# All 64 norms of a two-layer trunk: the epsilon added by ScalarE behind its Square, GpSimd left with the power

## The chip, the cores and the metric

The kernel runs on one core of a Trainium2 chip. The metric is the device time of one execution in microseconds (us), from start to end on that core. Each kernel is timed several times, and its median counts. A profiled execution gives the trace. Its span, from the first to the last recorded instruction, is slightly shorter than its device time. The engines are TensorE (PE, with its weight loads PEld), VectorE (DVE), ScalarE (ACT), GpSimd (POOL) and SyncE (SP), whose queue issues nearly all transfers.

## The reference

The reference is a trunk of two layers over x of shape (1, 1024, 1024) in float32, that is 1024 tokens of width 1024. Each layer is a mixer and a SwiGLU feed-forward network (FFN), and each of the four sub-layers has a norm ahead and a norm behind it:

```python
def rmsnorm(x, g):
    y = x * lax.rsqrt(jnp.mean(x * x, axis=-1, keepdims=True) + 1e-6)
    return y * g
# every sub-layer
x = x + rmsnorm(f(rmsnorm(x, g_pre)), g_post)
# layer 0: f = attention_mixer (8 heads chunked softmax, 8 heads stick-breaking, out-projection), then swiglu
# layer 1: f = recurrent_mixer (gated linear recurrence with a conv), then swiglu
def swiglu(h, w_gate, w_up, w_down):
    return (jax.nn.silu(h @ w_gate) * (h @ w_up)) @ w_down
```

The matrix products are made to float32 accuracy. The norms need, for each token, one number: (mean of squares + epsilon) to the power -1/2.

## The kernel before

**Tiles.** The 1024 tokens are eight tiles of 128 tokens, one token per partition, in the text "token 0" to "token 7". A norm of one tile makes a column of 128 numbers. With four sub-layers, two norms each and eight tiles, there are 64 such norms.

**One norm.** `rstd` (L170 to L184) computes it in three steps on two engines. ACT squares the tile with a scale of 1/32 and sums along the free axis into a column `ss` (L178; a second short instruction, ACTIVATION_READ_ACCUMULATOR, puts the sum out). POOL adds the epsilon, `rs` = `ss` + eps (L182). POOL raises `rs` to the power -0.5, with an exponent from a constant column `neghalf` (L183). In the last sub-layer four of the norms come in two halves of 512 columns. There the first half's sum gets the epsilon at L180, on POOL, and L182 adds the first half's column to the second's. `self.squared` names the last Square. Work that is to be issued behind a norm is tied to it (`last_m`, `behind`).

**Who uses it.** In `pre_norm` the normalized tile is either made by DVE together with the gain (L214, the attention's norm at the start, into `h`) or by ACT (L212, into `mg` or `m`; the gain is folded into the weights). Eight PE transposes of 128x128 then turn it (L222), and `sink.take` splits the result into a high and a low part (L57 and L58 into `hT` for a mixer, L85 to L96 into `hS` and `tf` for an FFN). In `post_norm_of` DVE multiplies the sub-layer's result by its gain (L250), and then one DVE instruction forms x = result * rs + x (L256). The new x is stored (L258) and, but for the last sub-layer, goes on into the next sub-layer's `pre_norm`.

**Stages.** The start normalizes and turns eight tiles of x while the attention's weights come in (PE L291 and L293 are its first products, on `psv`). At the end of a mixer the out-projection works through tokens 0 to 5 in threes and 6 and 7 at the end. The post-norms and the FFN's pre-norms of tokens 6 and 7 stand there between the last products and the first products of the FFN. The FFN's gate and up projections use Strassen's seven products (L604 to L661, tiles `q`, `c`, `first`). The down projection has six block products (L726 to L733 work on splits `o` of `raw` loads) and then a seventh over four tiles of tokens (L833 loads its weights `raw`; L842 and L843 split the loads `act`, which are small pieces of a stored activation `gA`). L848 ends it, tile by tile, and the post-norms of its two token groups run beside these products. The tile pools have few buffers (`act` 2, `x` 2, `rs` 4, `ss` 4), so a transfer into one waits until the former user is done.

**Order.** A scheduler sets the order of instructions on each engine, with a cost for each instruction and a simulated timeline. A changed instruction can therefore move others on all engines. Within an engine the order is fixed at build time, and each instruction waits for its inputs.

## Time and profile before

| | before |
|---|---|
| median of 3 runs | 2243.35 us (2241.7 to 2243.67) |
| profiled execution | 2241.47 us |
| its span | 2239.6 us |
| mean granted clock of PE | 0.995 |
| POOL, busy in the span | 227.3 us, 458 instructions |
| L183, the power, 64 times | 46.5 us, 727 ns each |

A row of the timeline reads: start in us, duration in us, engine, line, operation, output <- inputs (buffer numbers left out), how many in a row. In square brackets stand the idle time of the engine just before and what ended it. A row of a group reads: line, engine, operation, names, shapes, count, then busy us in total, the mean in ns, and the idle time before with its releasers. A row of PE's waits reads: what PE wanted, what it waited for, us in total, how many times, the longest. L numbers are lines of the kernel before.

### The profile page before, as it was taken

Reading aid. Unit: us, or ns where it says so; the run is one execution under the profiler, and the core shown is the slowest. Engines: PE = TensorE matmul, PEld = TensorE weight load, DVE = VectorE, ACT = ScalarE, POOL = GpSimd, SP = SyncE. Lnnn points to the kernel's source line nnn. Section 1 sums busy time; section 2 is a strip of 40 time slices with the busy share of each in tenths; the row PEclk is TensorE's granted clock in tenths of the full one; section 3 lists DMA queues with packets and bytes.
Section 4 is the critical chain, followed back from the end, with each engine's and each line's share of the span. In section 5 each row is a group of like instructions: output and inputs, shape, how many; then the busy total and the mean of one; then the engine's idle time right before and its main releaser. Section 6 shows DMA issues by size and latency. Waiting matters only on the chain. (4 is left out here: it accounts for less than half of the span.)

```text
span 2239.6 us, 30733 instructions
## 1 busy us (share of the span) xinstructions
PE 2194.9 (98%) x11198; PEld 1806.9 (81%) x11198; DVE 1539.4 (69%) x2496; ACT 1146.0 (51%) x2108; POOL 227.3 (10%) x458
## 2 busy tenths in 40 slices
PE   8999999999999999999999999999999999999997
PEld 8887888878788888888887777888788888888875
DVE  5776765464877777776767677437786777759665
ACT  4544455464765444432436576528655444425433
POOL 2111212131100000000001332202000000000011
PEclk9999999999999999999999999999999999999998
DMA  5101011125523323235558411356232323237466
GB/s 168 47 27 36 25 43 41 60 98 169 183 76 113 118 90 123 90 132 201 161 168 252 131 57 48 92 195 227 75 128 98 123 90 123 90 126 259 127 202 193
DMA packets 185978, 268.92 MB, mean 120 GB/s; under 512 B 13794, under 2 KB 115170, under 8 KB 185827
## 3 DMA queue, kind: packets, MB, share of 16 engines
q1 hardware_dynamic: 185186, 264.86, 37.5%
q10 hardware_dynamic: 640, 2.10, 0.3%
q8 instruction: 88, 1.44, 0.3%
q14 instruction: 64, 0.52, 0.1%
HBM read 201.38 MB, written 65.54 MB: 119 GB/s over the span
## 5 line engine op out<-in xcount | busy, mean ns | idle before, releaser
L646 PE MATMUL ps<-hS,q 128*128 128x512 f32 (+1 forms) x1288 | 489.7, 381 | 0.7 <-ACT hS L96 0.3
L647 PE MATMUL ps<-hS,q 128*128 128x512 f32 (+1 forms) x1288 | 489.0, 380 | 0.9 <-DVE hS L89 0.9
L648 PE MATMUL ps<-hS,q 128*128 128x512 f32 (+1 forms) x1288 | 488.4, 380 | 0.0
L617 DVE TENSOR_TENSOR q<-raw,q 128x512 fp32r<-128x512 f32 x308 | 204.5, 685 | 185.7 <-ACT q L616 185.2
L647 PEld LDWEIGHTS ps<-hS,q 128*128 128x128 f32 x1288 | 242.1, 188 | 47.5 <-DVE hS L89 1.3
L646 PEld LDWEIGHTS ps<-hS,q 128*128 128x128 f32 x1288 | 241.7, 188 | 47.8 <-ACT hS L96 0.7
L648 PEld LDWEIGHTS ps<-hS,q 128*128 128x128 f32 x1288 | 242.1, 188 | 45.8
L616 ACT CAST q<-raw 128x512 fp32r<-128x512 f32 x308 | 177.3, 616 | 154.7 <-DVE raw L625 127.6
L732 PE MATMUL ps<-o,o 128*128 128x512 f32 x616 | 241.6, 393 | 3.3 <-DVE o L727 3.2
L733 PE MATMUL ps<-o,o 128*128 128x512 f32 x616 | 238.8, 392 | 0.0
L731 PE MATMUL ps<-o,o 128*128 128x512 f32 x616 | 222.2, 395 | 10.1 <-ACT o L842 6.0
L604 ACT ACTIVATE raw<-raw,gcol 128x256 f32<-128x256 f32 x352 | 150.2, 498 | 151.8 <-DMA raw<-in_ffn_w_up_dram 73.2
L726 ACT CAST o<-raw 128x512 fp32r<-128x512 f32 x206 | 123.8, 620 | 197.7 <-PE ps L733 63.8
L727 DVE TENSOR_TENSOR o<-raw,o 128x512 fp32r<-128x512 f32 x206 | 138.0, 687 | 64.3 <-ACT o L726 63.4
L182 POOL TENSOR_SCALAR rs<-ss 128x1 f32<-128x1 f32 x60 | 33.1, 551 | 1451.5 <-ACT junk L178 1367.8
L731 PEld LDWEIGHTS ps<-o,o 128*128 128x128 f32 x616 | 116.2, 189 | 38.9 <-ACT o L842 8.5
L156 DVE TENSOR_TENSOR wlo<-raw,whi 128x1024 fp32r<-128x1024 f32 x76 | 93.1, 1225 | 71.5 <-ACT whi L155 70.1
L732 PEld LDWEIGHTS ps<-o,o 128*128 128x128 f32 x616 | 116.7, 189 | 29.5 <-DVE o L727 5.3
L733 PEld LDWEIGHTS ps<-o,o 128*128 128x128 f32 x616 | 116.6, 189 | 24.6 <-DVE o L843 0.7
L155 ACT CAST whi<-raw 128x1024 fp32r<-128x1024 f32 x76 | 79.7, 1051 | 58.7 <-PE ps L167 20.2
L401 ACT COPY pt<-tr 128x512 f32<-128x512 f32 (+1 forms) x128 | 65.5, 527 | 78.6 <-PE tr L397 78.0
L166 PE MATMUL psq<-hT,whi 128*128 128x512 f32 x256 | 101.2, 395 | 1.1 <-DVE v L296 1.1
(201 smaller groups left out, 4303.4 us busy)
## 6 DMA issues: line engine op xcount, KB each, us to landing
raw<-in_ffn_w_down_dram SPq DMA_DIRECT2D x96, 256.0 KB, 4.4
raw<-in_ffn_w_gate_dram SPq DMA_DIRECT2D x44, 512.0 KB, 4.2
raw<-in_ffn_w_up_dram SPq DMA_DIRECT2D x44, 512.0 KB, 4.2
gS<-c SPq DMA_DIRECT2D x88, 256.0 KB, 3.7
raw<-gS SPq DMA_DIRECT2D x88, 256.0 KB, 2.8
gA<-c SPq DMA_DIRECT2D x66, 256.0 KB, 3.5
raw<-in_attn_w_in_dram SPq DMA_DIRECT2D x24, 512.0 KB, 4.1
raw<-gA SPq DMA_DIRECT2D x44, 256.0 KB, 2.9
```

Source lines behind the costliest of these rows:

```text
L166: nc.tensor.matmul(ps, wh[:, kt, cols], hh[:, kt, :], start=kt == 0, stop=False)
L604: nc.scalar.activation(raw[:, i], raw[:, i], AF.Copy, scale=gain[:, 4 * k + i:4 * k + i + 1])
L616: self.last = nc.scalar.copy(t[:, 0], src).ins
L617: self.last_lo = nc.vector.tensor_tensor(t[:, 1], src, t[:, 0].bitcast(F32), op=ALU.subtract).ins
L646: nc.tensor.matmul(ps, a[:, 0, kt, :], bh, start=kt == 0, stop=False)
L647: nc.tensor.matmul(ps, a[:, 0, kt, :], bl, start=False, stop=False)
L648: self.matmul = nc.tensor.matmul(ps, a[:, 1, kt, :], bh, start=False, stop=kt == 3).ins
L726: nc.scalar.copy(t[:, 0], src)
L727: tt(t[:, 1], src, t[:, 0].bitcast(F32), op=ALU.subtract)
L731: nc.tensor.matmul(ps, a[0], b[:, 0], start=first, stop=False)
L732: nc.tensor.matmul(ps, a[0], b[:, 1], start=False, stop=False)
L733: nc.tensor.matmul(ps, a[1], b[:, 0], start=False, stop=last)
```

## The change

A constant column `eps` is made at the start. In `rstd` the add of POOL at L182 is replaced by an Identity activation on ACT: `rs` = `ss` + bias, with the bias from the `eps` column, or, for a norm in two halves, from the first half's column. The power stays on POOL. `self.squared` now names this activation and no longer the Square. The four adds at L180 stay on POOL.

```diff
         nc.vector.memset(self.neghalf, -0.5)
+        self.eps = c.tile([P, 1], F32, name="eps")
+        nc.vector.memset(self.eps, EPS)
...
             if i < len(parts) - 1:
                 nc.gpsimd.tensor_scalar(o, o, eps, None, op0=ALU.add)
                 eps = o
-        nc.gpsimd.tensor_scalar(rs, ss[-1], eps, None, op0=ALU.add)
+        self.squared = nc.scalar.activation(rs, ss[-1], AF.Identity, bias=eps if len(parts) > 1 else self.eps).ins
         nc.gpsimd.tensor_tensor(rs, rs, self.neghalf, op=ALU.pow)
```

In the changed kernel all lines behind L118 have numbers higher by 2, and so have the numbers in the tiles' names. The order of POOL loses 64 rows. ACT gains 64. The rows of DVE, PE and SP are the same but for the `eps` memset, in an order that differs at the start (ACT only), in the two out-projections' ends, and in the two down projections.

ACT at the start, where `h` and `ss` are the Square's outputs, `x` the tokens and `hT` the turned tokens. Before:

```order
L57 CAST hT_99<-pst_179 128x4x128
L57 CAST hT_99<-pst_184 128x4x128
L178 ACTIVATE h_201,ss_203<-x_122 128x1024
L178 ACTIVATE h_273,ss_275<-x_124 128x1024
L178 ACTIVATE h_294,ss_296<-x_126 128x1024
L57 CAST hT_99<-pst_208 128x4x128
L57 CAST hT_99<-pst_213 128x4x128
```

and now:

```order
L57 CAST hT_101<-pst_181 128x4x128
L57 CAST hT_101<-pst_186 128x4x128
L180 ACTIVATE h_203,ss_205<-x_124 128x1024
L180 ACTIVATE h_275,ss_277<-x_126 128x1024
L180 ACTIVATE h_296,ss_298<-x_128 128x1024
L184 ACTIVATE rs_204<-ss_205,eps 128x1
L184 ACTIVATE rs_276<-ss_277,eps 128x1
L184 ACTIVATE rs_297<-ss_298,eps 128x1
L57 CAST hT_101<-pst_210 128x4x128
```

The Identities of tokens 1, 2 and 3 stand together behind the third Square.

DVE at the end of the attention's out-projection, where `mg_6542` is token 7's result and `x_6543` its new x, `tf` and `hS` belong to an earlier token tile, and `first` to the FFN's first products. Before:

```order
L89 TENSOR_TENSOR tf_6369<-mg_6285,tf_6369 128x256
L89 TENSOR_TENSOR tf_6369<-tf_6369,mg_6285 128x256
L250 TENSOR_TENSOR mg_6542<-ps_6381,g_5889 128x1024
L256 SCALAR_TENSOR_TENSOR x_6543<-mg_6542,rs_6546,x_6543 128x1024
L89 TENSOR_TENSOR hS_5641<-tf_6369,hS_5640 128x16x64
L655 TENSOR_TENSOR first_6541<-ps_6609,first_6541 128x256
```

and now:

```order
L89 TENSOR_TENSOR tf_6371<-tf_6371,mg_6287 128x256
L252 TENSOR_TENSOR mg_6544<-ps_6383,g_5891 128x1024
L89 TENSOR_TENSOR hS_5643<-tf_6371,hS_5642 128x16x64
L657 TENSOR_TENSOR first_6543<-ps_6611,first_6543 128x256
L258 SCALAR_TENSOR_TENSOR x_6545<-mg_6544,rs_6548,x_6545 128x1024
```

The x of token 7 (L256, now L258) has moved behind the last `hS` of that earlier tile and behind the first operation on `first`.

PE in the final down projection, where `ps_19682` is the first token tile's product and `ps_19750` the second's, whose `act` load comes last. Before:

```order
L731 MATMUL ps_19682<-o_19632,o_19669 128x512
L731 MATMUL ps_19750<-o_19619,o_19737 128x512
L732 MATMUL ps_19750<-o_19619,o_19737 128x512
L732 MATMUL ps_19682<-o_19632,o_19669 128x512
L733 MATMUL ps_19682<-o_19632,o_19669 128x512
L731 MATMUL ps_19682<-o_19637,o_19674 128x512
```

and now:

```order
L733 MATMUL ps_19684<-o_19639,o_19676 128x512
L734 MATMUL ps_19684<-o_19639,o_19676 128x512
L735 MATMUL ps_19684<-o_19639,o_19676 128x512
L733 MATMUL ps_19684<-o_19643,o_19676 128x512
L733 MATMUL ps_19752<-o_19621,o_19739 128x512
L734 MATMUL ps_19752<-o_19621,o_19739 128x512
L734 MATMUL ps_19684<-o_19643,o_19676 128x512
```

The first two products of `ps_19750` have moved behind six more of `ps_19682`. On SP, in the same place, the load `act_19735` that they need has moved behind the load of the next token's x (`x_19786`). In the down projection of layer 0, SP has the weight load `raw_11711` ahead of `act_11799` instead of behind it.

## The prediction

> **What bounds the kernel now.** I read the page's first part and the chain of work first, then TensorE's waits, then the two GpSimd lines of the norm and ScalarE's short instructions, and last the timeline at every place where the order changed.

> ```profile
> PE 2194.9 (98%) x11198; PEld 1806.9 (81%) x11198; DVE 1539.4 (69%) x2496; ACT 1146.0 (51%) x2108; POOL 227.3 (10%) x458
> PE 23%; DMA 3%; DVE 2%; ACT 1%; issue 1%; SPq 0%; POOL 0%; POOLq 0%; DVEq 0%; ACTq 0%
> ```

> TensorE (PE) is busy for 98% of the span. GpSimd (POOL), from which the change takes work, is busy for 10% and has no visible share of the chain. So freeing POOL is not a gain in itself; only what shortens or lengthens a PE wait counts, or what lies behind the last matmul. The waits of PE, by what ended them (us in total, times, longest):

> ```profile
> PE ps L731 <- ACT o L842: 6.0, 4, 2.4
> PE pst L222 <- ACT mg L212: 5.3, 4, 2.0
> PE ps L732 <- DVE o L727: 3.2, 4, 2.5
> PE pst L222 <- DVE h L214: 2.5, 2, 2.3
> PE pst L222 <- ACT m L212: 1.1, 3, 0.5
> ```

> Norms end two rows of transposes directly (through L212: 5.3 + 1.1 us) and one through L214 (2.5 us, of which 2.29 us are the first norm's wait for its gain `g`). Were all waits on L212 to vanish, that is 6.4 us, 0.29%: the ceiling of any direct gain.

> **One norm: the price of the exchange.**

> ```profile
> L182 POOL TENSOR_SCALAR rs<-ss 128x1 f32<-128x1 f32 x60 | 33.1, 551 | 1451.5 <-ACT junk L178 1367.8 <-ACT mg L178 39.7 <-ACT m L178 26.7
> L212 ACT ACTIVATE mg<-x,rs 128x1024 f32<-128x1024 f32 x16 | 18.4, 1149 | 11.0 <-POOL rs L183 10.8
> L178 ACT ACTIVATE mg<-x 128x1024 f32<-128x1024 f32 x16 | 16.9, 1054 | 2.9 <-DVE x L256 2.9
> L869 ACT ACTIVATE l<-e 128x8 f32<-128x8 f32 x1 | 0.2, 208 | 0.0
> ```

> Removed: 64 adds at L182, 33.1 us for the 60 of one-part norms. Added: 64 Identity instructions of 128x1 with a per-partition bias on ScalarE (ACT). The trace has none of that shape. From below: the 128x8 row, 208 ns, by which the exchange would gain 0.09 us a norm. From above: the same plus what an operand read from a tile costs, 1149 - 1054 = 95 ns by L212 against L178, so 303 ns. I take the upper end, 0.30 us, since the bias is such an operand: 19 us in all, beside 1146 us on an engine that is half idle. [...]

> What the add costs on the path depends on VectorE (DVE):

> ```profile
> 14.17 0.81 POOL L182 TENSOR_SCALAR rs<-ss 128x1 f32<-128x1 f32 x1 [7.59 <-ACT h L178]
> 15.71 1.31 POOL L182 TENSOR_SCALAR rs<-ss 128x1 f32<-128x1 f32 x1
> 24.17 0.22 POOL L182 TENSOR_SCALAR rs<-ss 128x1 f32<-128x1 f32 x1
> 607.15 1.29 POOL L182 TENSOR_SCALAR rs<-ss 128x1 f32<-128x1 f32 x1 [4.83 <-ACT mg L178]
> 2232.66 0.28 POOL L182 TENSOR_SCALAR rs<-ss,ss 128x1 f32<-128x1 f32 x1 [2.23 <-ACT junk L178]
> 2233.03 0.57 POOL L183 TENSOR_TENSOR rs<-rs,neghalf 128x1 f32<-128x1 f32 x1
> ```

> Alone it takes 0.22 us; beside DVE instructions between SBUF tiles, as at 15.71 and 607.15, up to 1.3. Alone, one norm's chain stays as long as it was: 0.22 + 0.08 us to the pow go, 0.30 us of Identity come. Where the add stood held up, the pow arrives in its place and can be held up instead, so the gain lies between 0 and about 1.1 us. The DVE memset of the eps tile costs 0.06 us at the start, ahead of any wait.

> **The start, 8 norms.** In the new order the Identities of tiles 1, 2 and 3 stand behind the Squares of all three.

> ```profile
> 15.03 1.04 ACT L178 ACTIVATE h<-x 128x1024 f32<-128x1024 f32 x1
> 15.66 1.28 DVE L214 SCALAR_TENSOR_TENSOR h<-x,rs,g 128x1024 f32<-128x1024 f32 x1 [0.77 <-POOL rs L183]
> 17.10 1.07 PE L222 MATMUL pst<-ident,h 128*128 128x128 f32 x8 [0.18 <-DVE h L214]
> 19.66 0.38 PE L293 MATMUL psv<-whi,hT 128*128 128x256 f32 x1 [0.75 <-DVE hT L58]
> ```

> Tile 1's root was there at 15.63 (14.17 + add and pow). Now its Identity starts when the third Square has ended, 15.03 + 1.04 + 0.10 = 16.2, ends at 16.5, the pow at 17.1: L214 starts at 17.2 in place of 15.66, 1.5 us later. Tile 2's pow follows at once, so the next L214 starts as soon as DVE is free. PE's wait of 0.18 at 17.10 grows by 1.5, and the rows behind are as tight (0.75 at 19.66, bound by L58 on the same DVE), where part of it comes back since DVE now runs dense. I take **+1.2 us**, between 0.7 and 1.5.

> **Two out-projections, tokens 6 and 7.** Two tokens' transposes stand on PE's path in each layer (four waits, 5.3 us in the table above); those of the first layer:

> ```profile
> 610.48 1.09 PE L222 MATMUL pst<-ident,mg 128*128 128x128 f32 x8 [1.98 <-ACT mg L212]
> 618.14 1.09 PE L222 MATMUL pst<-ident,mg 128*128 128x128 f32 x8 [0.51 <-ACT mg L212]
> 613.12 1.28 DVE L256 SCALAR_TENSOR_TENSOR x<-mg,rs,x 128x1024 f32<-128x1024 f32 x1 [0.44 <-DVE mg L250]
> 614.33 1.22 DVE L89 TENSOR_TENSOR hS<-tf,hS 128x1024 fp32r<-128x1024 f32 x1
> 616.01 0.89 POOL L183 TENSOR_TENSOR rs<-rs,neghalf 128x1 f32<-128x1 f32 x1
> 615.46 0.42 DVE L655 TENSOR_TENSOR first<-ps,first 128x256 f32<-128x256 f32 x1
> ```

> Token 6: the Identity stands right behind its Square, the held-up add (607.15, 1.29) is gone, the pow takes some of its wait over: -0.4 us of the 1.98, between 0 and -1.1. Token 7: its post-norm's Identity stands behind two other ACT instructions, and DVE now has L89 (1.22) and L655 (0.42) ahead of L256, less the 0.44 it waited: 1.22 + 0.42 - 0.44 = 1.2 us later. Square, pow, L212 and the transposes follow one another, so the wait of 0.51 becomes 1.7, less the 0.3 us that an unimpeded pow (0.89 at this place, 0.57 alone) may give back: +0.9. Sum for a layer +0.5, **+1.0 us** for two; from -1.6 (tokens 6 at their best, tokens 7 unchanged) to +3.

> **Down projection of layer 0.** PE waits 1.04 and 2.27 us for `act` casts, whose loads SP issues late:

> ```profile
> 1225.73 0.50 PE L731 MATMUL ps<-o,o 128*128 128x512 f32 x1 [1.04 <-ACT o L842]
> 1233.87 0.74 PE L731 MATMUL ps<-o,o 128*128 128x512 f32 x1 [2.27 <-ACT o L842]
> 1226.21 0.38 SPq L196 DMA_DIRECT2D act<-gA  x1
> 1224.44 0.68 DVE L727 TENSOR_TENSOR o<-raw,o 128x512 fp32r<-128x512 f32 x1
> 1225.64 0.55 DVE L843 TENSOR_TENSOR o<-act,o 128x384 fp32r<-128x384 f32 x1
> ```

> The new order takes one weight load (`raw_11711`) ahead of the `act_11799` load on SP, while on DVE the 128x384 subtract at 1225.64, which frees an `act` buffer, moves ahead of three others of 0.6 us each (1224.44 to the next but one, 1225.64). The load at 1226.21 that waits for this buffer can so go up to 1.8 us sooner; the weight load in front of the other can take that back. I take 1.3 of the 1.8 off the waits: **-1.3 us**, from -3.9 (the long wait and the slow clock behind it, 2.27 + 1.6, below) to +1.2, were the weight load to hold SP for as long as that.

> **Final down projection.** DVE now does L256 of the first two tokens one L250 (1.21 us) sooner; their stores leave SP sooner, and the loads queued behind them too.

> ```profile
> 2167.39 1.21 DVE L250 TENSOR_TENSOR m<-m,g 128x1024 f32<-128x1024 f32 x1
> 2171.25 3.35 DMA out_dram<-x
> 2175.16 7.38 DMA x<-xs
> 2180.08 1.19 PE L731 MATMUL ps<-o,o 128*128 128x512 f32 x4 [2.04 <-ACT o L726]
> 2198.71 0.80 PE L731 MATMUL ps<-o,o 128*128 128x512 f32 x1 [2.38 <-ACT o L842]
> ```

> The chain of waits runs through that store, so the 2.04 us at 2180 shrink by up to 1.2; I take 1.0. PE now has six matmuls ahead of the first of `ps_19750`, some 1.4 us of cover for the 2.38; but the `act` load that ends it now stands on SP behind the next token's `x` load. I set these two against each other: **-1.0 us**, from -5.4 (1.0 and the second wait with the slow clock behind it, 2.38 + 2.0, below) to +1.4, were the cover to turn into waiting.

> **The tail.** Behind the last matmul are Square, add (2232.66 to 2232.94), pow at 2233.03. The Identity starts when the Square leaves ACT and ends near 2232.8: **-0.2 us**, between 0 and -0.3.

> **The sum.** 1.2 + 1.0 - 1.3 - 1.0 - 0.2 = -0.3 us. The profiled execution took 2241.47 us (span 2239.6 and 1.9 around it), hence 2241.2; the median of the three runs, 2243.35, is 1.9 above it, hence 2243.0 us. Differences within 0.2% (4.5 us) are about what a measurement of this kernel cannot tell from none.

> **The rivals.** *The clock falls.* Behind some waits PE runs at half speed (window, its us, PE busy and matmuls, granted clock, DMA share, GB/s):

> ```profile
> 1233.80:1237.30 3.50, 3.43 (x8) 0.52 0.32 92
> 2170.40:2175.00 4.60, 4.55 (x20) 1.00 0.85 211
> 2198.70:2203.20 4.50, 4.49 (x11) 0.50 1.04 315
> ```

> Waits of 1.98, 2.04 and 2.5 us (the last before 2170.40) kept the clock, 2.27 and 2.38 lost it; 8 and 11 matmuls at 0.43 and 0.41 us (3.43 / 8, 4.49 / 11) instead of 0.23 (4.55 / 20) cost 1.6 and 2.0 us. *Slower*: the price of token 7 is larger than my 1.2 us, its wait passes about 2.3 us in both layers and the clock goes. A layer then costs 1.9 + 2.0 - 0.4 (token 6) = 3.5 in place of 0.5; two of them put 6.0 on the sum, about 2249. That is the point from which it decides: a wait of 2.3 us. For it: the wait grows by a whole chain of four instructions on three engines. Against it: it would have to be 0.6 us more than the rows add up to, and 2.5 us kept the clock once.

> [...]

> *Faster*: both down projections lose their long wait and with it the slow stretch: 2.27 + 1.6 + 2.38 + 2.0 + 1.0 (at 2180) = 9.3 in place of 2.3, 7.0 off the sum, about 2236. For it: both waits get cover or earlier loads. Against it: `act_11799` is overtaken by a weight load on SP, the other `act` load by an `x` load.

> *The change does not do what it says*: the pow takes over the adds' wait for DVE and no chain gets shorter. Then tokens 6 and the tail give nothing: -0.3 + 0.8 + 0.2 = +0.7, 2244.0.

> **The numbers.** Shifts that stay within 4.5 us, the last rival (0.15 of it) among them: 0.68, with 2239.5 to 2246.5 as its own range. The clock rival 0.12, and 0.05 for two or more terms at their upper bounds: slower 0.17. The faster rival 0.11, and 0.04 for one down projection that loses its stretch while the start stays as it was: faster 0.15. The range from 2238 to 2248.5 leaves out the far part of both.

> **What would show it.** POOL's L182 row gone and 64 ACT rows of 128x1 at 0.2 to 0.33 us; pows of 1 us and more where the adds were held up; PE's wait of 0.18 at 17.1 grown to about 1.7; waits for token 6 at 1.6 and for token 7 near 1.4 in both layers; the waits near 1233 and 2178 smaller. I am wrong if a wait above 2.2 us with a granted clock of 0.5 behind it appears in an out-projection, or both such places in the down projections go.

## The result: 0.6% slower, and the profile after

| | before | after |
|---|---|---|
| median | 2242.52 us (4 runs) | 2254.16 us (4 runs) |
| range | 2237.16 to 2243.67 | 2251.59 to 2256.34 |
| ratio | | 1.0058, 95% interval 1.0045 to 1.0071 |
| profiled execution, span | 2241.47, 2239.6 | 2256.34, 2254.5 |

The forecast was 2243.0 us, "the same", with a range to 2248.5. The kernel is some 12 us slower and lies outside the range.

The first part of the page after, and PE's waits (what PE wanted, what it waited for, us in total, times, longest):

```profile
PE 2210.7 (98%) x11198; PEld 1810.3 (80%) x11198; DVE 1540.4 (68%) x2497; ACT 1162.5 (52%) x2172; POOL 201.5 (9%) x394
```

```profile
PE pst L224 <- ACT mg L214: 9.0, 4, 2.6
PE ps L734 <- DVE o L729: 4.6, 5, 2.5
PE pst L224 <- DVE h L216: 3.8, 2, 2.2
PE ps L733 <- ACT o L844: 3.6, 4, 1.6
PE ps L733 <- ACT o L728: 2.6, 2, 1.6
PE pso L408 <- ACT pt L403: 2.5, 2, 2.2
```

The span grew by 14.9 us and PE's busy time by 15.8 (2194.9 to 2210.7), with the same 11198 matmuls. PE does not wait longer: all rows of this view together are 32.4 us after and 33.6 before. So the loss does not lie in the waits, which the prediction was made of. PE runs more slowly while it is busy.

Two stretches in which PE never waits show where. The first lies among the last projections of the recurrent mixer, the second in the second FFN's gate and up products. The columns are the window, its us, PE busy with the number of matmuls, granted clock, DMA share and GB/s. Before, then after:

```profile
1420.00:1480.00 60.00, 60.00 (x267) 1.00 0.33 96
1900.00:1960.00 60.00, 60.00 (x266) 1.00 0.30 96
```

```profile
1420.00:1480.00 60.00, 60.00 (x260) 1.00 0.32 97
1900.00:1960.00 60.00, 60.00 (x266) 1.00 0.37 114
```

At a granted clock of 1.00 in all four rows, the mixer's window holds 260 matmuls where it held 267. The 267 are all of L166 to L168. Of the 260, 226 are of these lines and 34 of L944 to L946 (by the lines of before), which keep their pace, so the count even understates the slowing. The FFN gets 266 in both. The busy share of 100% says nothing of this; the count beside it does.

I paired every matmul's start with the one of the same number in the other trace and sorted the 11197 differences of their distances by what stood between the two starts. Matmuls of 512 columns follow one another, at full clock, at these medians (ns, by the kernel before's lines):

| | L166 to L168 | L497 | L646 to L648 | L731 to L733 |
|---|---|---|---|---|
| before | 227 | 227 | 227 | 227 |
| after | 232 to 233 | 234 | 227 | 227 |

Summed over the execution, the pace made some 10 us of the 14.8 by which the last matmul started later, waits made about -2, and stretches of half clock 6.6. (Where a longer distance starts to count as a wait moves the first two by up to 1 us.) The last term belongs to this one execution more than to the kernel (below).

**What moved.** The lines that lost pace have one operand on each side of SBUF. The tiles of the `const`, `main` and most other pools lie from the low end upwards. `hT` (the moving operand of L166 to L168) and `ah`, `al` (the stationary one of L497) are in pools allotted from the high end downwards. The column `eps` takes 4 bytes in each partition, but in the built kernels a tile takes at least 32. In the built kernel every tile allotted on the low side behind it lies 32 bytes higher, modulo 256 (with the new order some took another buffer besides); those of the high side stay (but for two small columns in each of two pools, which change places). L646 to L648 and L731 to L733 have both operands on the low side, and they keep their distance.

### The profile page after: what moved, and what is told of

The parts are those of the page before. It is cut to its first block, busy times and chain, and to the rows that moved or that the text cites. A ratio compares the mean times of both kernels' runs of the same rounds, so it can differ in the third digit from the quotient of the medians.

```text
span 2254.5 us, 30732 instructions
## 1 busy us (share of the span) xinstructions
PE 2210.7 (98%) x11198; PEld 1810.3 (80%) x11198; DVE 1540.4 (68%) x2497; ACT 1162.5 (52%) x2172; POOL 201.5 (9%) x394
## 4 chain that ended last, share of the span: by engine, by line
PE 81%; DMA 6%; DVE 5%; ACT 4%; issue 2%; SPq 1%; POOL 1%; POOLq 0%; DVEq 0%; ACTq 0%
PE ps L648 12%; PE ps L649 12%; PE ps L650 12%; PE ps L499 6%; PE pso L408 3%; PE tr L399 3%; PE ps L733 3%; PE ps L734 3%; PE ps L735 3%; PE psq L168 3%; PE psq L169 3%; PE psq L170 3%; PE ps L169 2%; PE ps L170 2%; PE ps L168 2%
## 5 line engine op out<-in xcount | busy, mean ns | idle before, releaser
L648 PE MATMUL ps<-hS,q 128*128 128x512 f32 (+1 forms) x1288 | 489.9, 381 | 0.0
L649 PE MATMUL ps<-hS,q 128*128 128x512 f32 (+1 forms) x1288 | 489.5, 380 | 0.0
L619 DVE TENSOR_TENSOR q<-raw,q 128x512 fp32r<-128x512 f32 x308 | 205.2, 685 | 176.8 <-ACT q L618 176.2
L649 PEld LDWEIGHTS ps<-hS,q 128*128 128x128 f32 x1288 | 242.7, 188 | 46.4 <-DVE q L619 0.5
L648 PEld LDWEIGHTS ps<-hS,q 128*128 128x128 f32 x1288 | 242.4, 189 | 46.0 <-issue 0.5
L733 PE MATMUL ps<-o,o 128*128 128x512 f32 x616 | 222.8, 396 | 6.3 <-ACT o L844 3.6
L185 POOL TENSOR_TENSOR rs<-rs,neghalf 128x1 f32<-128x1 f32 x64 | 55.7, 874 | 1515.4 <-ACT rs L184 1506.8
L733 PEld LDWEIGHTS ps<-o,o 128*128 128x128 f32 x616 | 117.2, 191 | 33.8 <-ACT o L844 5.1
L168 PE MATMUL psq<-hT,whi 128*128 128x512 f32 x256 | 102.2, 399 | 1.1 <-DVE v L298 1.1
```

The costliest lines, as they stand in the source:

```text
L168: nc.tensor.matmul(ps, wh[:, kt, cols], hh[:, kt, :], start=kt == 0, stop=False)
L619: self.last_lo = nc.vector.tensor_tensor(t[:, 1], src, t[:, 0].bitcast(F32), op=ALU.subtract).ins
L648: nc.tensor.matmul(ps, a[:, 0, kt, :], bh, start=kt == 0, stop=False)
L649: nc.tensor.matmul(ps, a[:, 0, kt, :], bl, start=False, stop=False)
L733: nc.tensor.matmul(ps, a[0], b[:, 0], start=first, stop=False)
```

## The experiments

Theory A: the slower pace comes from the 32 bytes between the two sides. Rival B: the new order and the Identities make the loss. Rival C: the pace varies from run to run.

**The tile alone** (order of all engines as before):

```diff
+        self.spare = c.tile([P, 1], F32, name="spare")
         self.zero = c.tile([P, 1], F32, name="zero")
```

> The kernel before with one more constant column of 128x1 (never written or read) in the place where the change puts eps; every engine's order is the same as before, but tiles allocated on the left of SBUF lie 32 bytes higher, those on the right stay. Theory A (addresses): the pace of the out-projection's matmuls (L497) goes from 227 to 234 ns and that of L166 to L168 from 227 to 232 to 234, with 8 to 12 us in all: 2250 to 2254. Rival B (order and the Identities): no change from before, 2243 within 3, pace 227. Rival C (the pace varies from run to run): either, without regard to the address.

Measured: 2249.26 against 2238.2 us of before on that chip, ratio 1.0046 (1.0031 to 1.0061). The two windows:

```profile
1420.00:1480.00 60.00, 60.00 (x259) 1.00 0.28 86
1900.00:1960.00 60.00, 60.00 (x267) 1.00 0.37 117
```

A column that nothing writes or reads costs 10 us and slows the same matmuls. (The first window holds 249 of them and 10 of L944 to L946.) Without one Identity and in the old order, most of the loss is there: B cannot have that part.

**The high side moved as well, the change kept.**

```diff
-        ... tc.tile_pool(name="edge", bufs=1, side="right")).tile([P, 48], F32, name="edge")
+        ... tc.tile_pool(name="edge", bufs=1, side="right")).tile([P, 56], F32, name="edge")
```

> The changed kernel with the unused tile edge at the right end of SBUF made 8 floats wider, so that the tiles on the right also move by 32 bytes; order as in the changed kernel. Theory A with the relative position as its cause: pace back at 227 ns, time 8 to 12 us below the changed kernel, 2242 to 2247. Theory A with the absolute position of the left tiles as its cause: pace stays at 232 to 234, 2254. Rival B: 2254.

Measured: 2250.59 us, ratio 1.0057 (1.0042 to 1.0072). I had the sign wrong. The high side is filled downwards, so a wider `edge` put `hT` 32 bytes lower, and the distance grew to 64 bytes instead of going back to nothing. Read so, it agrees with A, with L166 to L168 at 233 ns.

**64 bytes by a second column** (the `spare` line above, in the changed kernel).

> The changed kernel with a second unused column behind eps, so that the left tiles lie 64 bytes higher than before instead of 32. Theory A: if what counts is the position within 64 bytes, pace 227 ns and 2242 to 2247; if it is the position within 128 or more, pace above 227 and 2250 to 2256. Rival B: 2254, pace 232 to 234.

Measured: 2248.01 us, ratio 1.005 (1.0033 to 1.0068); L166 to L168 at a mean of 233 ns, L497 at 230. A distance of 64 is no cure.

**Both sides moved, no change** (the `spare` column and the wider `edge` in the kernel before; here too the distance became 64).

> The kernel before with the unused column of the first of these runs and the wider edge tile as well: left tiles 32 bytes up, right tiles 32 bytes down, order as before. Theory A, relative position: as before, 2243 within 3, pace 227. Theory A, absolute position: 2250 to 2254. Rival B: as before.

Measured: 2247.72 us, ratio 1.0038 (1.0026 to 1.0049), pace as in the last one. Four kernels, two with the order of before and two with that of the change, have the slow pace in the same lines.

**The change without a new tile**, the decisive one:

```diff
-        self.neghalf = c.tile([P, 1], F32, name="neghalf")
+        both = c.tile([P, 2], F32, name="neghalf")
+        self.neghalf, self.eps = both[:, 0:1], both[:, 1:2]
...
-        self.eps = c.tile([P, 1], F32, name="eps")
```

> The changed kernel with eps as a second element of the neghalf column's tile, so that no other tile moves; order as in the changed kernel. Theory A (addresses): pace of all matmuls of 512 columns back at 227 ns, and what is left is the change itself: the ratio to before between 0.999 and 1.003, by the slow-clock stretches that the new waits set off. Rival B (the new order and the Identities carry the loss): 1.005 to 1.006, as the changed kernel.

Measured: 2244.39 against 2241.88 us, ratio 1.0005 (0.9994 to 1.0015).

```profile
1420.00:1480.00 60.00, 60.00 (x267) 1.00 0.31 90
1900.00:1960.00 60.00, 60.00 (x266) 1.00 0.33 106
```

All 64 Identities, the new order, and 267 matmuls in the window again: no difference that this comparison resolves. B falls as the cause of the loss; a remainder of up to 0.15% is left open by the interval.

**Which distances are dear** (the kernel before with `spare` of 24, 32 and 64 floats).

> The kernel before with an unused column group of 96 bytes: left tiles up by 96, order as before. Theory A, pace set by the distance of the two operands modulo 256 bytes: proj (distance 96) and out-projection (160) at paces not seen yet, 230 to 234 if every distance but 0 is dear; 2245 to 2251. A pace below 227 would show that 0 is not the best distance.

> The kernel before with an unused column group of 128 bytes: left tiles up by 128, order as before. Theory A: if the pace repeats every 128 bytes, 227 ns and the time of before; if it repeats every 256 only, 230 to 234 ns and 7 to 11 us above before.

> The kernel before with an unused column group of 256 bytes: left tiles up by 256, order as before. Theory A with a period of 256 bytes: pace 227 ns for all and the time of before, ratio within 0.2% of 1. If any shift of the left tiles against the right ones is dear, 232 to 234 ns and 1.004 to 1.005. Rival C (pace varies from run to run): either.

Measured: 2259.15 us with 96 bytes and 2248.23 with 128, one run each (the first is above the 2251 that I had as its upper end, and with one run the reason stays open); 2241.61 with 256, ratio 0.9995 (0.9985 to 1.0006). With 256 bytes, the pace of before:

```profile
1420.00:1480.00 60.00, 60.00 (x266) 1.00 0.31 97
```

Taking from the built kernels the address of each matmul's moving operand and that of the next one's stationary operand, and from the traces the mean distance between the two starts (512 columns, full clock):

| stationary minus moving, modulo 256 bytes | mean ns | from |
|---|---|---|
| 0 | 227 | all lines before; 256 bytes moved |
| 32 | 233.2 | L166 to L168, 32 bytes |
| 64 | 233.3 | L166 to L168, 64 bytes |
| 96 | 234.1 | L166 to L168, 96 bytes |
| 128 | 232.8 | both lines, 128 bytes |
| 160 | 233.4 | L497, 96 bytes |
| 192 | 230.3 | L497, 64 bytes |
| 224 | 233.3 | L497, 32 bytes |

A shift changes the distance with opposite signs in the two lines, since L166 has its stationary operand on the low side and L497 its moving one. Of these distances only 0, a multiple of 256, keeps 227 ns. Some 40 matmuls of L364 and L365 are an exception: they take 231 to 232 ns at distance 0, before and after alike, and the runs do not show why. Rival C falls with the eight traces: the pace follows the address in each.

**Another pair of operands** (before, order as before):

```diff
         with pool("s0") as sp:
+            sp.tile([P, 8], F32, name="pad_s0")
```

and the same in `s1`.

> The kernel before with 32 unused bytes ahead of hS in the FFN's pool: hS and the tiles behind it (c, and the q of six of seven up products) lie 32 bytes higher, the q of the gate products and of one up product stay, and so does everything else; order as before. Theory A, the distance of the two operands modulo 256 bytes: the gate's matmuls and a seventh of the up's (8 of 14, some 2200 of L647 to L649's 3864) go from 227 to 233 ns, the other up products and all other matmuls stay at 227; 13 to 14 us more, near 2255. If only hT and the out-projection's tiles were sensitive: no change.

Measured: 2253.86 against 2240.24 us, ratio 1.006 (1.0041 to 1.0078). Before and this one, in the first FFN, then this one in the mixer's projections and in the second FFN:

```profile
700.00:740.00 40.00, 40.00 (x178) 1.00 0.33 99
```

```profile
700.00:740.00 40.00, 40.00 (x175) 1.00 0.34 105
1420.00:1480.00 60.00, 60.00 (x266) 1.00 0.32 97
1900.00:1960.00 60.00, 60.00 (x261) 1.00 0.36 110
```

Now the FFN's products are slow (266 became 261, since only part of the second window's matmuls are affected) and the projections are not. Of the matmuls of 512 columns at full clock, the 1943 whose distance became 224 have a mean of 233.3 ns, the 5727 others 227.2. It was no property of `hT`. This kernel also shows which two operands count. In 22 matmuls the distance to their own stationary operand is 224 and that to the next matmul's is 0: they have 227.1 ns. In 22 others it is the other way round: 235.0 ns. So in this kernel the pace follows the stationary operand of the next matmul, whose load of 0.19 us the trace shows beside this one.

**Part by part, without a shift.** Identity for the 24 norms inside the down projections alone:

```diff
-        nc.gpsimd.tensor_scalar(rs, ss[-1], eps, None, op0=ALU.add)
+        if self.in_down:
+            self.squared = nc.scalar.activation(rs, ss[-1], AF.Identity, bias=...).ins
+        else:
+            nc.gpsimd.tensor_scalar(rs, ss[-1], eps, None, op0=ALU.add)
```

> Without any shift of tiles: Identity on ScalarE for the 24 norms inside the two down projections, GpSimd's add for the 40 others. From the waits of the unshifted change against before (down projections 4.5 us less, out-projections 4 us more, start 1 more): start and out-projections as before, the gain of the down projections left, 2 to 5 us under before, ratio 0.998 to 0.999, if the order there stays as in the change and slow-clock stretches do not take it back; otherwise 1.000.

Measured: 2241.26 against 2240.24 us, ratio 1.0004 (0.9995 to 1.0013). The gain that I expected is not there. And the opposite, `if not self.in_down`:

> Without any shift of tiles: Identity for the 40 norms at the start and in the two out-projections, GpSimd's add for the 24 inside the down projections. By the same waits 5 us over before, ratio 1.002 to 1.003; PE's waits for tokens 6 and 7 as in the unshifted change (2.6 and 1.9 to 2.2), those of the down projections as before.

Measured: 2244.38 us, ratio 1.0015 (1.0006 to 1.0024). The start and the out-projections cost something, less than the 5 us expected. Token 6 waited 2.60 us in both layers, as expected. Token 7 waited 0.41 and 0.73 us, not 1.9, and yet its transposes stood as far behind token 6's as in the full change (8.73 us in the first layer in both, 7.66 before): PE merely had 8.3 us of its other work in between where it had 6.8. So the size of that one wait does not tell what the delay costs.

**The change with its own tile, and the high side moved the right way** (`edge` of 40 floats in place of 48, so that both sides lie 32 bytes higher).

> The changed kernel, eps as its own tile, with the unused tile edge made 8 floats narrower instead of wider: the tiles on the right move up by 32 bytes as those on the left do, so all addresses differ from before but no distance between the two sides does. Order as in the changed kernel. Theory A, distance modulo 256 bytes: pace 227 ns, ratio 0.999 to 1.002, as with eps in the neghalf tile. Theory A with absolute positions, or rival B: 1.005 to 1.006.

Measured: 2244.05 against 2239.59 us, ratio 1.0014 (1.0005 to 1.0024).

```profile
1420.00:1480.00 60.00, 60.00 (x266) 1.00 0.32 91
```

The addresses of both operands differ from before, their distance does not, and the pace is back: it is the distance, not the position. With this, the change itself costs between -1 and 5 us by the two intervals (around 1.0005 and 1.0014), and the tile's place some 10 us. No version beat the kernel before.

In the kernel before the distance is 0 modulo 256 in all its matmuls of 512 columns. The size of the unused tile `edge` at the high end sets it between the two sides.

## Why the prediction was wrong

**The step that failed** is the one sentence on the new column: "The DVE memset of the eps tile costs 0.06 us at the start, ahead of any wait." I costed the instruction and not the tile. It moves its neighbours, and two groups of matmuls that nobody touched became some 2.5% slower. By the paces, 1473 matmuls by 233.2 - 227.8 and 663 by 233.3 - 227.4 ns are 11.9 us; the tile alone measured 10.3 us (0.0046 of 2242). No rival had it, so the range could not reach it. Taking the tile's place out, the change is at 1.0005 to 1.0014 by the two kernels, 2243.6 to 2245.7 us by the median of before: "the same", as forecast. That agreement is in part luck, since by the list below one term has the wrong sign, waits that went had no term, and the tail hardly gained.

The other steps, by the trace after:

- **The price of an Identity**: estimated at 0.30 us, measured 290 ns.

```profile
L184 ACT ACTIVATE rs<-ss,eps 128x1 f32<-128x1 f32 x60 | 16.9, 290 | 0.8
L185 POOL TENSOR_TENSOR rs<-rs,neghalf 128x1 f32<-128x1 f32 x64 | 55.7, 874 | 1515.4 <-ACT rs L184 1506.8 <-DVE o L729 8.4
```

- **The pow inherits the hold-up**: its mean goes from 727 to 874 ns. Of what the adds took on POOL, 9.2 us came back there (46.5 to 55.7). Beside DVE's rows of L619 and L89 from 614.15 to 616.30 one took 2.17 us; in the trace before, at 2233.03 with DVE idle, it is 0.57.
- **The start**: the wait of 0.18 us grew to 1.60 (forecast 1.7), the one behind it shrank from 0.75 to 0.22, as the sum had it. From PE's wait for the first norm to that for `v` it is 52.68 - 10.08 = 42.60 us in place of 52.42 - 10.45 = 41.97, 0.6 longer; I had +1.2, between 0.7 and 1.5. Before, then after:

```profile
10.45 0.69 PE L222 MATMUL pst<-ident,h 128*128 128x128 f32 x2 [2.29 <-DVE h L214]
52.42 0.47 PE L166 MATMUL psq<-hT,whi 128*128 128x512 f32 x1 [1.08 <-DVE v L296]
```

```profile
10.08 0.69 PE L224 MATMUL pst<-ident,h 128*128 128x128 f32 x2 [2.17 <-DVE h L216]
18.08 1.07 PE L224 MATMUL pst<-ident,h 128*128 128x128 f32 x8 [1.60 <-DVE h L216]
20.11 0.38 PE L295 MATMUL psv<-whi,hT 128*128 128x256 f32 x1 [0.22 <-DVE hT L58]
52.68 0.47 PE L168 MATMUL psq<-hT,whi 128*128 128x512 f32 x1 [1.10 <-DVE v L298]
```

- **Tokens 6 and 7**: mis-sized. PE's row for token 7 of the second layer before, then the rows of both layers after, and POOL's for token 6:

```profile
1590.43 1.09 PE L222 MATMUL pst<-ident,mg 128*128 128x128 f32 x8 [0.81 <-ACT mg L212]
```

```profile
617.48 1.09 PE L224 MATMUL pst<-ident,mg 128*128 128x128 f32 x8 [2.60 <-ACT mg L214]
626.21 1.09 PE L224 MATMUL pst<-ident,mg 128*128 128x128 f32 x8 [1.89 <-ACT mg L214]
1596.29 1.09 PE L224 MATMUL pst<-ident,mg 128*128 128x128 f32 x8 [2.60 <-ACT mg L214]
1605.01 1.33 PE L224 MATMUL pst<-ident,mg 128*128 128x128 f32 x7 [1.89 <-ACT mg L214]
```

```profile
614.08 2.17 POOL L185 TENSOR_TENSOR rs<-rs,neghalf 128x1 f32<-128x1 f32 x1 [5.05 <-ACT rs L184]
```

  Token 6 was to gain 0.4 us; its wait grew from 1.98 to 2.60. The add and pow took 2.1 us there (607.15 to 609.24), and the pow alone now takes 2.17, with the Identity in front. The rival "the pow takes over the adds' wait" held in full at this place, and the Identity came on top. Token 7 went from 0.51 to 1.89 (forecast 1.4) and in the other layer from 0.81 to 1.89. The sum of these waits is 2 x 0.62 + 1.38 + 1.08 = 3.7 us where I had 1.0. Against it stand waits behind them, at the FFN's first products, that I had not counted. Before they are

```profile
PE ps L647 <- DVE hS L89: 0.9, 2, 0.4
PE ps L646 <- ACT hS L96: 0.3, 2, 0.2
```

  and the view after has no such row: 1.2 us less.

- **The down projections**: PE's waits for `o` are theirs alone. Before, they are the 6.0 and 3.2 us of the prediction's rows and this one:

```profile
PE ps L731 <- ACT o L726: 4.0, 4, 2.0
```

  13.2 us in all; after, 3.6 + 4.6 + 2.6 = 10.8 by the rows at the top. That is 2.4 us less, forecast 2.3, though not where I had it: in the first one PE waited 1.04 and 2.27 us before and 1.60 and 1.56 after, by nearly the same sum.

```profile
1232.03 0.50 PE L733 MATMUL ps<-o,o 128*128 128x512 f32 x1 [1.60 <-ACT o L728]
1234.52 0.79 PE L733 MATMUL ps<-o,o 128*128 128x512 f32 x1 [1.56 <-ACT o L844]
```

- **The tail** hardly gained: from the last Square's start to that of the last x it is 1.79 us after (2246.73 to 2248.52) and 1.86 before (2231.77 to 2233.63), 0.07 less where I had 0.2.
- **The clock rival** came in part. In the two kernels that keep the distance, the mean granted clock was 0.9923 and 0.9927 (10 and 11 runs), against 0.9938 and 0.9939 for before on the same chips. Taking a lost share of the clock for the same share of the time (an estimate), that is 3.4 and 2.7 us of 2243, where the ratios give 1.1 and 3.1: about what the change itself costs. It did not need the wait of 2.3 us that I had set as its point. After, the waits of 2.60 kept the clock in both layers, and in the second one it went behind token 7's 1.89:

```profile
1596.30:1599.70 3.40, 3.40 (x29) 1.00 0.19 64
1605.50:1608.90 3.40, 3.40 (x18) 0.50 0.00 0
```

  One of the readings that gave me that point was off, too: the slow stretch that I put down to the wait of 2.38 us (2196.3 to 2198.7) began at 2196.5, 0.2 us into that wait and behind 1.4 us of idle in the 3.40 us from 2193.10 (PE busy for 2.02 of them), so that wait alone did not bring it about.

## What to carry to other kernels

Here a column of 4 bytes moved the tiles behind it on its side by 32 bytes, and that cost some 10 us: compare addresses of matmul operands before and after, as one compares the order of instructions. When the loss is not in the waits, count matmuls in windows that are 100% busy at full clock: here the count was 260 for 267 in 60 us, while the busy share stayed at 100%. And when work is taken from an engine because it is held up there beside another engine's work, look at what comes next on that engine: here the pow waited in the add's place (727 to 874 ns).

## What the runs showed of the hardware

**Stretches of half clock lay on a grid.** They lasted 3.4, 6.8 or 10.2 us in all traces (but for the last one, which runs on to the end) and began, in each trace, on one grid of 3.41 us: before, two of them began at 8.58 and 1233.96 us, 359 times 3.4133 apart. The same wait of 1.98 us for token 6 kept the clock before and lost it in the kernel with Identity in the down projections only. Before (the wait from 608.50 to 610.48), then that kernel (608.17 to 610.15), the window with the wait and the one behind it:

```profile
607.10:610.50 3.40, 1.42 (x13) 1.00 0.95 287
610.50:613.90 3.40, 3.40 (x29) 1.00 0.28 96
```

```profile
607.80:611.20 3.40, 1.42 (x13) 1.00 0.95 292
611.20:614.60 3.40, 3.40 (x18) 0.50 0.02 8
```

In the second, the wait lies within one window of that trace's grid, and the next one runs at half clock, with 18 matmuls for 29. Before, a boundary of the grid (1233.96 less 183 times 3.4133, that is 609.3) cut it in two. Over the 14 traces, at full clock and by the matmuls' modelled ends, all of some 40 windows with 1.95 us or more of idle were followed by a half-clock one, none of some 65 with 0.8 to 1.2 us, and 17 or 18 of some 60 in between. So in these traces the place of a wait on the grid counted beside its length; a half-clock stretch of one window cost some 1.7 us, an estimate from its granted clock of 0.50 and its 3.41 us. The runs of the unchanged kernel spread over 9 us on one chip (2238.21 to 2247.31, 19 runs of before); how much of that lies in the grid was not shown.
